# An encoder layer on one core: where w_out's right operands are split, and how the merge's weights and heads are fed

## The chip, the cores and the metric

The kernel runs on one core of one Trainium2 chip. The metric is the time of one execution on the device, in microseconds (us). Engines are called PE (TensorE matmuls; PEld is its weight load), DVE (VectorE), ACT (ScalarE), POOL (GpSimd) and SP (SyncE, which here only issues transfers).

## The reference, cut to what matters

One layer over a sequence of 1024 positions and 1024 channels, in float32: a SwiGLU feed-forward block, a mixer with two branches, a second SwiGLU block, and a final norm.

```python
def reference(x, ...):
    x = x + 0.5 * swiglu(rms_norm(x, ffn1_norm), ffn1_wg, ffn1_wu, ffn1_wd)   # D_FF = 2816
    x = x + hybrid_mixer(rms_norm(x, mix_norm), ...)
    x = x + 0.5 * swiglu(rms_norm(x, ffn2_norm), ffn2_wg, ffn2_wu, ffn2_wd)
    return rms_norm(x, final_norm)

def hybrid_mixer(h, ...):
    u_f, q, k, v, g_a, g_b = split(h @ w_in)
    y_a = fourier_branch(u_f) @ w_fourier_out          # real part of a 2-D DFT per group
    o = diff_attention(q, k, v, positions, rel_bias, lam)   # softmax(s1) - lam * softmax(s2), 4 heads
    y_b = rms_norm(o, subln_g).reshape(...) @ w_attn_out
    merged = sigmoid(g_a) * y_a + sigmoid(g_b) * y_b
    return merged @ w_out
```

## The kernel before, in words

**Products.** Every float32 matrix product is made of three passes of the array: each operand is split into a rounded high part and a low part that holds the rest, and the kernel multiplies high by high, high by low and low by high. A split is two instructions (`split`, L131 to L134): a copy into the high part on ACT (L133) and a subtraction into the low part on DVE or POOL (L134). Where a block of four by four tiles is multiplied, seven products of sums and differences take the place of eight. `seven_products` (L389) does so for projections: left operands come from a stream of weights, right operands are the normed activations that stay on chip. `Lower` (L455) does so for the products that add to the residual: the two down-projections and w_out. One of its steps is twelve matmuls of 128x512.

**The stream of weights.** `Stream` (L150) holds a list of loads and preparations in order. `get` (L180) hands out the next prepared operand and runs ahead: five loads and two preparations past the one handed out, but not past the first entry of `stops`. `stop()` puts such a mark at the end of the list as it stands, `open()` takes the first mark away. The marks are: one after the first FFN's weights (L708, opened in `done1`, L1171), one after the eight pieces of w_attn_out (L1668, opened in `done2`, L1886), one after the second FFN's weights. A prepared operand lies in a tile called op, of which there are four (L136). A loaded block lies in a tile called r2 (shown as r in the trace), of which there are fourteen. A tile is free when its last reader is done.

**Lower.** `prep` (L539) makes the two operands of one step: the left one is a sum of activations, the right one a block of weights or a sum of blocks that was put into memory earlier (`sums_d`). `land` (L511) starts the right block's load up to six steps ahead, into spare quarters of the n tiles; `prep` splits it into an operand slot. There are twelve slots, two to a step: eight halves of the tiles n2, n3, n12, n13 and four op tiles (`slots`, `open_ext` L527, `slot` L533). For w_out, `LAST` (L40) names the products whose splits subtract on POOL: left of P4, P2 and P3, right of P2; P2 and P3 are the closing ones.

**Stages.** Input norm; first up-projection (`ffn`, L825: 11 blocks of hidden columns, two times seven products of twelve matmuls each); first down-projection; projections of the mixer with heads 0 and 1 beside them; heads 2 and 3 with the Fourier branch beside them (loop at L1783, g from 18); the merge `y_b` (L1817: for each of 16 outputs, twelve matmuls against w_attn_out, then a gate); w_out (`low.run`, L1895); second up-projection and down-projection; final norm.

**Beside the first up-projection** three generators are stepped once a product. `right_sums` (L734) makes the sums of right blocks of the down-projection and then those of w_out (order given at L1164). `bias_prepare` (L987) makes the position bias. `mixer_weights` (L767) splits the Fourier weights and, one piece every five products, w_attn_out, loads and stores of 0.25 and 0.5 MB a piece; it is stepped in the third to the ninth block of hidden columns, 98 products.

**Heads and merge.** `head_prep` (L1254) loads each half of q and k twice through the tile rh (three of them) and splits it; `combine` (L1332) scales one softmax by the other's factor, on DVE for odd blocks of heads 2 and 3 and on ACT and POOL for even ones; `turn` (L1344), `weigh` (L1362), `back` (L1376) and `head_norm` (L1420) follow. In `fourier` (L1442) a DVE and an ACT instruction write the two interleaved halves of one tile, DVE first (L1559, L1561). Before the last head is normed, the first four outputs of the merge are started with the heads that are ready. Pieces of w_attn_out come as ready operands through the stream, on ACT's queue (L1661 to L1668).

**Order of the work.** A planner orders each engine's instructions when the kernel is built: it runs a simulated time line, takes the first ready instruction in program order, and gives tiles out as they come free. `in_order` pins an instruction behind the one before it on its engine. On the chip each engine then follows its list.

```python
def get(self, prep=None):
    prep = self.PREP if prep is None else prep          # 2
    self.ahead(self.used + 1, self.used + 1)
    self.ahead(self.used + 1 + self.LOAD, self.used + 1 + prep)   # LOAD = 5
```

Of the kernel before, what the change touches and what calls it, by code (L numbers as in the profile page):

```python
# [27 lines left out]
H = 4  # L28
# [8 lines left out]
FOURIER_STEPS = 40  # L37
EARLY = ("34", "156", "016", "01"), ("34", "", "016", "01"), ("4", "4", "01", "")
DRAINS = {4: {(0, 2): 1, (1, 1): 3, (1, 2): 3, (1, 3): 3}, NP: {(n, j): 1 for n in range(2) for j in range(2 - n, 11 - n, 2)}}
LAST = ("P4", "P2", "P3"), ("P2",)  # L40
NBLK = 7
HEAD_ROWS = P * (PITCH + 1) + 64
SCALE = 1.0 / np.sqrt(float(S * P))
# [5 lines left out]
def encoder_layer(ctx: ExitStack, tc: tile.TileContext, a: dict, out: bass.AP):  # L49
# [405 lines left out]
    class Lower:  # L455
# [55 lines left out]
        def land(self):  # L511

            while self.landing < min(self.prepared + self.LAND, len(self.steps)):
                c, q, j, u = self.steps[self.landing]
                name = self.ORDER[q]
                srcs = [u["right"][name]]
                if self.spills and q >= 5:
                    srcs.insert(0, u["far"][q - 5])
                if len(store[self.where(c, q)]) < len(srcs):
                    return  # L520
                self.landing += 1
                pieces = [take(self.where(c, q)) for _ in srcs]
# [16 lines left out]
        def prep(self):  # L539

            self.land()
            c, q, j, u = self.steps[self.prepared]
            self.prepared += 1
            name = self.ORDER[q]
            a = [p and p[1] for p in u["a"]]

            def add(y, op, v, w):
                dve.tensor_tensor(out=y, in0=v, in1=w, op=op)

            if name == "P1" and u["raw"]:  # L550
                add(a[2], ALU.subtract, a[0], a[2])
            if name == "P5":
                add(a[0], ALU.add, u["s"], a[0])
            pieces = self.landed.pop(0)
            if len(pieces) == 1:
                left = self.LEFT[name]
                pieces.insert(0, ("s", u["s"]) if left == "s" else u["a"][left])
            ops = []
            for (_, src), names in zip(pieces, LAST):
                key, o = self.slot(q >= 5)  # L560
                split(src, o[:, 0, :], o[:, 1, :], pool if name in names and not self.spills else dve)
                ops.append((key, (o[:, 0, :], o[:, 1, :])))
            self.ops.append(ops)
            give(pieces[1])
# [12 lines left out]
            self.pump(2)  # L577
# [176 lines left out]

    attn_d = dram.tile([DT, P, 2, 512], F32, name="attn_d")
    cx_d = dram.tile([P, 2, 512], F32, name="cx_d")
    cw_d = dram.tile([4, P, 4, 2, 256], F32, name="cw_d")
    three = {}

# [7 lines left out]
    def mixer_weights():  # L767
# [29 lines left out]
        for q in range(4):  # L797
# [15 lines left out]
                yield  # L813
                in_order(sp.dma_start(out=cw_d[q][:, 2 * i:2 * i + 2], in_=t.bitcast(F32)))
            yield
        for dm in range(DT):
            r, o = htile(dm % 2 * 2, [P, 512], F32), htile(dm % 2 * 2 + 1, [P, 2, 512])
            in_order(sp.dma_start(out=r, in_=a["w_attn_out"][dm]))
            for _ in range(4):
                yield  # L820
            parts(r, o[:, 0, :], o[:, 1, :])
            yield
            in_order(sp.dma_start(out=attn_d[dm], in_=o.bitcast(F32)))

    def ffn(k, x_src, each, beside, also=None, third=None):  # L825

# [327 lines left out]
    def each1():  # L1154
# [5 lines left out]
        if n == 9:  # L1160
            bank_list.clear()
        drain(1 if n < 9 else 2)

    low = ffn(1, a["x"], each1, right_sums([(down(1, j), sums_d[1][j]) for j in (*range(SPILL, NP), *range(SPILL))]  # L1164
                                           + [(outward(j), sums_d["o"][j]) for j in range(4)]), bias_prepare(), mixer_weights())
    state = {}

    def done1(t, x, r):
# [64 lines left out]
    def twice(src):  # L1233

        r = rh()
        for half in (L, U):
            sp.dma_start(out=r[half, :], in_=src)
        return r
# [8 lines left out]
    def k_split(h, c, hh, r):  # L1247

        hs = slice(hh * HS, (hh + 1) * HS)
        kh, kl = stk[h][2 + c][:, hs], stk[h][4 + c][:, hs]  # L1250
        in_order(act.activation(kh, r, AF.Copy))
        pool.tensor_tensor(out=kl, in0=r, in1=kh, op=ALU.subtract)

    def head_prep(h):  # L1254

        if h == 3:
            two = [ntile(4 + j, [P, 2, S]) for j in range(2)]
            stk[h] = [two[j // 2][:, j % 2, :] for j in range(4)] + [xtile(5, [P, S], F32R)]
        else:
# [10 lines left out]
        r = None  # L1270
        for fn, t in ((q_split, h), (k_split, 4 + h)):
            for hh in range(2):
                if r is not None:
                    for c in range(2):
                        due[0](h, c, due[1], r[c])
                r = [twice(proj_d[t][(L, U)[c], hh * HS:(hh + 1) * HS]) for c in range(2)]
                due = fn, hh
                yield
        for c in range(2):
            due[0](h, c, due[1], r[c])  # L1280
        r = load_v(0)
        yield
# [49 lines left out]
    def combine(g):  # L1332
# [2 lines left out]
        dve.reciprocal(out=cc, in_=l2s[:, g:g + 1])  # L1335
        dve.tensor_scalar(out=cc, in0=cc, scalar1=l1s[:, g:g + 1], scalar2=nlam, op0=ALU.mult, op1=ALU.mult)
        s1, s2 = sc[g]
        if g % 2 == 1 and g >= G0:
            dve.scalar_tensor_tensor(out=s1, in0=s2, scalar=cc, in1=s1, op0=ALU.mult, op1=ALU.add)
        else:  # L1340
            act.activation(s2, s2, AF.Copy, scale=cc)  # L1341
# [100 lines left out]
    def fourier():  # L1442
# [72 lines left out]
        for n_, j in enumerate(order):  # L1515
# [37 lines left out]
            if n_ + 1 < len(order):  # L1553
# [2 lines left out]
            af = r2()  # L1556
            af2 = af.rearrange("p (k two) -> p two k", two=2)
            q = 0 if even else 1
            dve.scalar_tensor_tensor(out=af2[:, q], in0=alt, scalar=quarter, in1=ps[:, q * 256:(q + 1) * 256],  # L1559
                                     op0=ALU.mult, op1=ALU.add)  # L1560
            act.activation(af2[:, 1 - q], ps[:, (1 - q) * 256:(2 - q) * 256], AF.Copy)  # L1561
            if j == 0:
                stack(A[0][:, 0, :], af, (A[0][:, 0, :], A[0][:, 1, :]), three["x"])
            else:
# [93 lines left out]
                    sp.dma_start(out=ya_d[dm, :, hs], in_=y)  # L1658
                yield

    def fetch_op(src):  # L1661
        o = op_tile()
        act.dma_start(out=o.bitcast(F32), in_=src)
        return o[:, 0, :], o[:, 1, :]
# [91 lines left out]
    def prefetch(n):  # L1756
# [11 lines left out]
        for k in range(n):  # L1768
            ready.append(inputs(k // 2, k % 2, where))

    fgen = fourier()
    hgen = head_prep(3)
    NG = H * TT
# [9 lines left out]
    for g in range(G0 + 2, NG + 2):  # L1783
# [28 lines left out]


    todo = [(dm, hh) for dm in range(DT) for hh in range(2)]
    wa = {}

    def y_b(n_, ps, heads):  # L1817

        dm, hh = todo[n_]
        if dm not in wa:  # L1820
            wa[dm] = ws.get()
# [8 lines left out]
    for _ in head_norm(H - 1, (0,)):  # L1830
        pass

    first4 = []
    for n_ in range(4):
        if n_ % 2 == 0:
            two = banks2()
        first4.append(two[:, n_ % 2 * 512:(n_ % 2 + 1) * 512])
        y_b(n_, first4[n_], range(H - 1))
    back(NG - 2)
    head_scale(NG - 2, NG)  # L1840
    for _ in head_norm(H - 1, (1,)):
        pass
    units = [{"a": [None] * 4, "raw": True, "right": rights(outward(j), sums_d["o"][j])} for j in range(4)]
# [6 lines left out]
    for n_, (dm, hh) in enumerate(todo):  # L1850
        while len(ready) < min(n_ + 9, len(todo)):
            ready.append(inputs(*todo[len(ready)]))
        if n_ < 4:
            ps = first4[n_]
            y_b(n_, ps, (H - 1,))
        else:
            ps = bank("bp"[n_ % 2])
# [184 lines left out]
```

## Time and profile before

| | |
|---|---|
| Median of 3 runs | 2035.76 us (2034.42 to 2037.39) |
| The profiled execution | 2035.69 us, of which the span of instructions is 2033.9 us |
| PE busy | 1953.8 us of the span (96%), 9460 matmuls |
| DVE, ACT, POOL busy | 1409.7, 1000.8, 629.8 us |
| Moved | 341.60 MB |

The span runs from the first instruction to the last; 1.8 us of the profiled execution lie around it. Busy time is the time in which an engine executes; a matmul's end is modelled. The idle time before an instruction is put down to what released it.

### The profile page before, as it was taken

Reading aid. Unit: us, or ns where it says so; the run is one execution under the profiler, and the core shown is the slowest. Engines: PE = TensorE matmul, PEld = TensorE weight load, DVE = VectorE, ACT = ScalarE, POOL = GpSimd, SP = SyncE. Lnnn points to the kernel's source line nnn. Section 1 sums busy time; section 2 is a strip of 40 time slices with the busy share of each in tenths; the row PEclk is TensorE's granted clock in tenths of the full one; section 3 lists DMA queues with packets and bytes.
Section 4 is the critical chain, followed back from the end, with each engine's and each line's share of the span. In section 5 each row is a group of like instructions: output and inputs, shape, how many; then the busy total and the mean of one; then the engine's idle time right before and its main releaser. Section 6 shows DMA issues by size and latency. Waiting matters only on the chain. (4 is left out here: it accounts for less than half of the span.)

```text
span 2033.9 us, 27633 instructions
## 1 busy us (share of the span) xinstructions
PE 1953.8 (96%) x9460; PEld 1635.3 (80%) x9460; DVE 1409.7 (69%) x2165; ACT 1000.8 (49%) x1804; POOL 629.8 (31%) x477
## 2 busy tenths in 40 slices
PE   6999999999999999999998898998999999999998
PEld 5887888888888878888886786877888888888886
DVE  7777767649767846656657886868766654578765
ACT  7434344334355645867756653356333333344454
POOL 6533223220000354344375540057322323300010
PEclk9999999999999999999999899999999999999999
DMA  4567956419426353344358668433655432166335
GB/s 135 195 211 254 318 199 224 156 50 333 145 78 214 116 163 122 119 140 139 104 162 278 194 207 301 143 104 95 211 200 189 150 119 73 53 218 227 104 102 173
DMA packets 205216, 341.60 MB, mean 168 GB/s; under 512 B 22101, under 2 KB 63069, under 8 KB 204561
## 3 DMA queue, kind: packets, MB, share of 16 engines
q1 hardware_dynamic: 197792, 324.35, 48.3%
q10 hardware_dynamic: 5760, 12.59, 1.7%
q0 software_dynamic: 1520, 2.88, 0.5%
q8 instruction: 74, 1.21, 0.3%
q14 instruction: 70, 0.57, 0.1%
HBM read 249.53 MB, written 94.40 MB: 169 GB/s over the span
## 5 line engine op out<-in xcount | busy, mean ns | idle before, releaser
L405 PE MATMUL p<-n,op 128*128 128x512 f32 (+1 forms) x5256 | 1151.5, 378 | 21.4 <-DVE op L134 7.3
L405 PEld LDWEIGHTS p<-n,op 128*128 128x128 f32 x5256 | 944.9, 190 | 207.0 <-DVE op L134 8.8
L217 POOL TENSOR_TENSOR r<-r,r 128x512 f32<-128x512 f32 x252 | 361.2, 1440 | 885.9 <-DVE op L134 507.8
L134 DVE TENSOR_TENSOR op<-r,op 128x512 fp32r<-128x512 f32 x427 | 356.9, 840 | 282.6 <-ACT op L133 271.6
L133 ACT ACTIVATE op<-r 128x512 fp32r<-128x512 f32 x446 | 277.9, 627 | 290.6 <-PE p L405 198.2
L607 PE MATMUL b<-n 128*128 128x512 f32 x996 | 237.4, 391 | 0.9 <-DVE r L1860 0.9
L607 PEld LDWEIGHTS b<-n 128*128 128x128 f32 x996 | 187.2, 188 | 40.3 <-ACT op L133 1.3
L417 ACT ACTIVATE r<-p 128x512 f32<-128x512 f32 (+1 forms) x138 | 74.1, 537 | 124.3 <-PE p L405 121.6
L607 PE MATMUL b<-op,op 128*128 128x512 f32 x528 | 129.3, 391 | 2.7 <-DVE op L134 2.7
L607 PEld LDWEIGHTS b<-op,op 128*128 128x128 f32 x528 | 99.4, 189 | 23.7 <-DVE op L134 3.1
L421 DVE TENSOR_TENSOR r<-p,r 128x512 f32<-128x512 f32 (+1 forms) x138 | 85.0, 616 | 40.3 <-PE p L405 37.0
L133 ACT ACTIVATE n<-n 128x512 fp32r<-128x512 f32 x126 | 74.7, 621 | 68.5 <-PE b L607 22.3
L134 DVE TENSOR_TENSOR n<-n,n 128x512 fp32r<-128x512 f32 x118 | 82.3, 716 | 32.1 <-ACT n L133 32.1
L607 PE MATMUL p<-n 128*128 128x512 f32 x336 | 80.1, 390 | 0.0
L1914 POOL TENSOR_TENSOR r<-r,x 128x512 f32<-128x512 f32 x5 | 7.7, 1559 | 224.3 <-ACT r L1913 224.3
L607 PEld LDWEIGHTS p<-n 128*128 128x128 f32 x336 | 62.9, 188 | 13.0
L1342 POOL TENSOR_TENSOR x<-x,x 128x1024 f32<-128x1024 f32 x16 | 38.4, 2398 | 101.4 <-ACT x L1341 101.4
L607 PE MATMUL p<-op,op 128*128 128x512 f32 x288 | 68.3, 391 | 0.0
L607 PEld LDWEIGHTS p<-op,op 128*128 128x128 f32 x288 | 53.8, 188 | 11.0
L133 ACT ACTIVATE op<-n 128x512 fp32r<-128x512 f32 x66 | 39.3, 621 | 35.3 <-PE b L607 13.9
L1327 DVE CUSTOM_DVE_ANT_0 x<-A,x 128x1024 f32<-128x1024 f32 x32 | 39.0, 1219 | 20.2 <-PE b L1358 13.4
L133 ACT ACTIVATE n<-x 128x512 fp32r<-128x512 f32 x48 | 30.0, 630 | 42.8 <-PE b L607 33.1
(336 smaller groups left out, 2454.3 us busy)
## 6 DMA issues: line engine op xcount, KB each, us to landing
kx<-in_ffn_wd SPq DMA_DIRECT2D x118, 256.0 KB
r<-in_ffn_wg SPq DMA_DIRECT2D x96, 256.0 KB
r<-in_ffn_wu SPq DMA_DIRECT2D x94, 256.0 KB
n<-sums_d SPq DMA_DIRECT2D x88, 256.0 KB
sums_d<-kx SPq DMA_DIRECT2D x66, 256.0 KB
proj_d<-r SPq DMA_DIRECT2D x56, 256.0 KB
h_d<-x SPq DMA_DIRECT2D x16, 512.0 KB
rh<-proj_d SPq DMA_DIRECT2D x64, 128.0 KB
```

The costliest lines, as they stand in the source:

```text
L133: act.activation(hi, src, AF.Copy)
L134: eng.tensor_tensor(out=lo, in0=src, in1=hi, op=ALU.subtract)
L217: pool.tensor_tensor(out=b[o], in0=b[x], in1=b[y], op=op)
L405: pe.matmul(ps, lhsT=w[wi][:, d * P:(d + 1) * P], rhs=xn[b][xi][:, d, cols], start=(first and m == 0), stop=(last and m == 11), skip_group ...
L417: act.activation(o, view(p), AF.Copy)
L421: dve.tensor_tensor(out=o, in0=view(p), in1=o, op=ALU.add)
L607: pe.matmul(ps[p], lhsT=wa[ai][:, p * P:(p + 1) * P], rhs=wb[bi], start=(j == 0 and m == 0 and name in self.FRESH), stop=False, skip_group ...
L1327: dve.tensor_tensor_reduce(out=dst, in0=ps, in1=bt, scale=-0.125, scalar=3.0e38, op0=ALU.add, op1=ALU.min, accum_out=nmx)
L1342: pool.tensor_tensor(out=s1, in0=s2, in1=s1, op=ALU.add)
L1914: pool.tensor_tensor(out=y[1], in0=y[1], in1=gain[1][1], op=ALU.mult)
```

## The change

- w_out's right operands (28: four units of seven products) are split beside the first up-projection, in `mixer_weights`, and stored as both parts in `out_d`, 0.5 MB each. In the w_out stage a right operand is loaded straight into its slot (in `prep`, on SP's queue), with no split there. All left operands of w_out are split on ACT and DVE; `LAST` goes.
- The pieces of w_attn_out and w_out, 36 in all, go through that generator one to a product, with loads two pairs ahead. So that w_out's sums are there, `right_sums` makes them first.
- w_attn_out's pieces no longer come through the stream: `fetch_wa` loads six of them in the attention loop (four into op tiles, two into x4 and kx) and the last two in the merge, on SP's queue. The stream's entries for them and the mark after them go.
- Six outputs of the merge are started before the last head is normed, in place of four.
- `head_prep`: k is loaded over its whole width into the tile where its low part will stand and split in place; q's halves and k's are split in turn.
- `combine`: for heads 2 and 3 all blocks on DVE. `fourier`: the ACT copy stands ahead of the DVE instruction.

```diff
-LAST = ("P4", "P2", "P3"), ("P2",)
@@ Lower.land
-                srcs = [u["right"][name]]
+                srcs = [] if "both" in u else [u["right"][name]]
@@ Lower.prep
-            if len(pieces) == 1:
+            if len(pieces) < 2:
...
-            for (_, src), names in zip(pieces, LAST):
+            for i in range(2):
                 key, o = self.slot(q >= 5)
-                split(src, o[:, 0, :], o[:, 1, :], pool if name in names and not self.spills else dve)
+                if i < len(pieces):
+                    split(pieces[i][1], o[:, 0, :], o[:, 1, :])
+                else:
+                    sp.dma_start(out=o.bitcast(F32), in_=u["both"][q])
                 ops.append((key, (o[:, 0, :], o[:, 1, :])))
@@ mixer_weights
-        for dm in range(DT):
-            r, o = htile(dm % 2 * 2, [P, 512], F32), htile(dm % 2 * 2 + 1, [P, 2, 512])
-            in_order(sp.dma_start(out=r, in_=a["w_attn_out"][dm]))
-            for _ in range(4):
+        jobs = [(a["w_attn_out"][dm], attn_d[dm]) for dm in range(DT)]
+        for j in range(4):
+            b = rights(outward(j), sums_d["o"][j])
+            jobs += [(b[name], out_d[j, n]) for n, name in enumerate(Lower.ORDER)]
+        def load_two(n):
+            t = htile(n % 2 * 2, [P, 2, 512], F32)
+            for q in range(2):
+                in_order(sp.dma_start(out=t[:, q, :], in_=jobs[2 * n + q][0]))
+            return t
+        ahead = [load_two(0), load_two(1)]
+        yield
+        yield
+        for n in range(len(jobs) // 2):
+            t = ahead.pop(0)
+            for q in range(2):
+                o = htile(2 * q + 1, [P, 2, 512])
+                parts(t[:, q, :], o[:, 0, :], o[:, 1, :])
                 yield
-            parts(r, o[:, 0, :], o[:, 1, :])
-            yield
-            in_order(sp.dma_start(out=attn_d[dm], in_=o.bitcast(F32)))
+                in_order(sp.dma_start(out=jobs[2 * n + q][1], in_=o.bitcast(F32)))
+            if n + 2 < len(jobs) // 2:
+                ahead.append(load_two(n + 2))
@@ head_prep, k_split
-        in_order(act.activation(kh, r, AF.Copy))
-        pool.tensor_tensor(out=kl, in0=r, in1=kh, op=ALU.subtract)
+        in_order(act.activation(kh, kl.bitcast(F32), AF.Copy))
+        pool.tensor_tensor(out=kl, in0=kl.bitcast(F32), in1=kh, op=ALU.subtract)
...
+        r = load_q(0)
+        for c in range(2):
+            twice(proj_d[4 + h][(L, U)[c], :], stk[h][4 + c].bitcast(F32))
...
@@ combine
-        if g % 2 == 1 and g >= G0:
+        if g >= G0:
@@ fourier
+            act.activation(af2[:, 1 - q], ps[:, (1 - q) * 256:(2 - q) * 256], AF.Copy)
             dve.scalar_tensor_tensor(out=af2[:, q], in0=alt, scalar=quarter, in1=ps[:, q * 256:(q + 1) * 256],
                                      op0=ALU.mult, op1=ALU.add)
-            act.activation(af2[:, 1 - q], ps[:, (1 - q) * 256:(2 - q) * 256], AF.Copy)
@@ the stream
-    for dm in range(DT):
-        ws.add(None, lambda dm=dm: fetch_op(attn_d[dm]))
-    ws.stop()
     order_ffn(2)
@@ the attention loop
+        if g == G0 + TT + 2:
+            fetch_wa(0, 1, 2, 3)
+            fetch_wa(4, 5, homes=[xtile(4, [P, 2, 512], F32R), T(big, "kx", [P, 2, 512], F32R, 2)])
@@ the merge
-    for n_ in range(4):
+    for n_ in range(6):
...
+        first.append(two[:, n_ % 2 * 512:(n_ % 2 + 1) * 512] if n_ < 4 else bank("p"))
...
+        if n_ == 3:
+            fetch_wa(6, 7)
```

where

```python
def fetch_wa(*dms, homes=None):
    for n, dm in enumerate(dms):
        o = op_tile() if homes is None else homes[n]
        sp.dma_start(out=o.bitcast(F32), in_=attn_d[dm])
        wa[dm] = o[:, 0, :], o[:, 1, :]
```

## Rows read from the trace of the kernel before

**Rows 1.** Windows: busy us (count) of PE, PEld, DVE, ACT, POOL; clock, DMA share, GB/s.

```profile
220.00:320.00 100.00, 98.98 (x434) 80.69 (x433) 68.49 (x89) 37.73 (x67) 30.04 (x21) 1.00 0.73 256
320.00:440.00 120.00, 120.00 (x531) 99.38 (x530) 77.73 (x99) 47.98 (x81) 37.78 (x26) 1.00 0.40 135
1040.00:1240.00 200.00, 178.06 (x990) 150.00 (x989) 150.12 (x281) 116.15 (x214) 100.67 (x101) 0.96 0.67 214
1240.00:1292.00 52.00, 43.22 (x183) 34.37 (x182) 39.25 (x67) 9.84 (x18) 0.00 (x0) 0.90 0.83 301
1292.00:1377.00 85.00, 81.53 (x367) 66.61 (x366) 59.40 (x83) 41.98 (x86) 32.69 (x22) 0.98 0.31 107
```

**Rows 2.** PE's time line: start, duration, line, out<-in, count [idle before <-releaser].

```profile
1073.08 4.14 PE L405 MATMUL p<-n,op 128*128 128x512 f32 x10 [3.78 <-DVE op L134]
...
1135.85 0.69 PE L1382 MATMUL b<-ident,rh 128*128 128x128 f32 x2 [8.04 <-ACT rh L1374]
...
1250.14 0.63 PE L1431 MATMUL b<-ident,rh 128*128 128x128 f32 x4 [2.27 <-DVE rh L1428]
...
1265.73 2.90 PE L1825 MATMUL b<-x,op 128*128 128x512 f32 x6 [5.17 <-DMA op<-attn_d]
...
1270.99 1.73 PE L1825 MATMUL p<-x,op 128*128 128x512 f32 x6
...
1273.94 1.52 PE L1825 MATMUL b<-x,op 128*128 128x512 f32 x6
...
1276.66 1.52 PE L1825 MATMUL p<-x,op 128*128 128x512 f32 x6
...
1362.36 1.20 PE L607 MATMUL b<-op,op 128*128 128x512 f32 x4 [2.67 <-DVE op L134]
```

**Rows 3.** The merge weights' stores and loads: durations min/median/max in ns, first and last.

```profile
L823 SPq DMA_DIRECT2D attn_d<-h x8: 326/354/417, 234.3 to 330.3; - x8
L1663 ACTq DMA_DIRECT2D op<-attn_d x8: 326/326/346, 1081.0 to 1265.2; - x8
```

**Rows 4.** Groups by line, 120 to 400 us: busy us, mean ns, idle before.

```profile
L134 DVE TENSOR_TENSOR op<-r,op 128x512 fp32r<-128x512 f32 x100 | 83.5, 836 | 48.7 <-ACT op L133 47.8
L133 ACT ACTIVATE op<-r 128x512 fp32r<-128x512 f32 x101 | 63.3, 628 | 86.7 <-PE p L405 70.0 <-issue 8.7 <-POOL r L217 7.6
```

**Rows 5.** DVE's time line in the last projection and beside the heads.

```profile
1066.97 7.25 DVE L134 TENSOR_TENSOR op<-r,op 128x512 fp32r<-128x512 f32 x3 [6.91 <-ACT op L133]
...
1129.65 4.33 DVE L134 TENSOR_TENSOR x<-r,x 128x512 fp32r<-128x512 f32 x1
1133.91 0.47 DVE L1559 SCALAR_TENSOR_TENSOR r<-r,r,p 128x256 f32<-128x256 f32 x1
```

**Rows 6.** ACT's time line: the wait for a head's load, and the merge weights' issues.

```profile
1063.04 0.63 ACT L1244 ACTIVATE x<-rh 128x512 fp32r<-128x512 f32 x1 [4.20 <-DMA rh<-proj_d]
...
1080.96 0.33 ACTq L1663 DMA_DIRECT2D op<-attn_d  x1
...
1084.12 0.33 ACTq L1663 DMA_DIRECT2D op<-attn_d  x1
```

**Rows 7.** The Fourier copy's line: its wait on ACT's queue, in ns.

```profile
L1561 ACTq EVENT_SEMAPHORE  x1: 9787/9787/9787, 1124.6 to 1124.6; - x1
```

**Rows 8.** Groups by line, 1080 to 1240 us: combine on POOL, DVE and ACT.

```profile
L1342 POOL TENSOR_TENSOR n<-n 128x1024 f32<-128x1024 f32 x8 | 19.2, 2403 | 16.2 <-ACT n L1341 16.2
...
L1339 DVE SCALAR_TENSOR_TENSOR n<-n,ccs 128x1024 f32<-128x1024 f32 x8 | 13.7, 1708 | 0.2
...
L1341 ACT ACTIVATE n<-n,ccs 128x1024 f32<-128x1024 f32 x8 | 9.2, 1148 | 0.6 <-DVE ccs L1336 0.6
```

**Rows 9.** The DVE form of combine, by its line: ns min/median/max, first and last start.

```profile
L1339 DVE SCALAR_TENSOR_TENSOR n<-n,ccs x8: 1275/1286/3075, 1092.9 to 1215.5; 128x1024 f32<-128x1024 f32 x8
```

**Rows 10.** Groups by line in the w_out stage, 1292 to 1377 us.

```profile
L134 POOL TENSOR_TENSOR op<-n,op 128x512 fp32r<-128x512 f32 x8 | 11.9, 1506 | 23.6 <-ACT op L133 23.6
...
L377 DVE SCALAR_TENSOR_TENSOR h<-h,col,x 128x512 f32<-128x512 f32 x8 | 10.3, 1356 | 0.0
```

More of the change, by code (lines that the diff above doesn't have):

```diff
@@ L558, in prep @@
             ops = []
-            for (_, src), names in zip(pieces, LAST):
+            for i in range(2):
                 key, o = self.slot(q >= 5)
-                split(src, o[:, 0, :], o[:, 1, :], pool if name in names and not self.spills else dve)
+                if i < len(pieces):
+                    split(pieces[i][1], o[:, 0, :], o[:, 1, :])
+                else:
+                    sp.dma_start(out=o.bitcast(F32), in_=u["both"][q])
                 ops.append((key, (o[:, 0, :], o[:, 1, :])))
             self.ops.append(ops)
-            give(pieces[1])
+            for piece in pieces[1:]:
+                give(piece)
             if name in ("P5", "P4", "P2", "P3") or name == "P7" and self.spills:
@@ L756, in encoder_layer @@
     cx_d = dram.tile([P, 2, 512], F32, name="cx_d")
+    out_d = dram.tile([4, NBLK, P, 2, 512], F32, name="out_d")
     cw_d = dram.tile([4, P, 4, 2, 256], F32, name="cw_d")
@@ L1162, in each1 @@
         drain(1 if n < 9 else 2)
-    low = ffn(1, a["x"], each1, right_sums([(down(1, j), sums_d[1][j]) for j in (*range(SPILL, NP), *range(SPILL))]
-                                           + [(outward(j), sums_d["o"][j]) for j in range(4)]), bias_prepare(), mixer_weights())
+    low = ffn(1, a["x"], each1, right_sums([(outward(j), sums_d["o"][j]) for j in range(4)] +
+                                           [(down(1, j), sums_d[1][j]) for j in (*range(SPILL, NP), *range(SPILL))]),
+              bias_prepare(), mixer_weights())
     state = {}
@@ L1231, in encoder_layer, with twice @@
     L, U = slice(0, 64), slice(64, 128)
-    def twice(src):
-        r = rh()
+    def twice(src, r):
         for half in (L, U):
@@ L1245, in q_split, with k_split @@
         pool.tensor_tensor(out=q[lo, :], in0=r[lo, :], in1=q[lo, :], op=ALU.subtract)
-    def k_split(h, c, hh, r):
+    def k_split(h, c, hh):
         hs = slice(hh * HS, (hh + 1) * HS)
         kh, kl = stk[h][2 + c][:, hs], stk[h][4 + c][:, hs]
-        in_order(act.activation(kh, r, AF.Copy))
-        pool.tensor_tensor(out=kl, in0=r, in1=kh, op=ALU.subtract)
+        in_order(act.activation(kh, kl.bitcast(F32), AF.Copy))
+        pool.tensor_tensor(out=kl, in0=kl.bitcast(F32), in1=kh, op=ALU.subtract)
     def head_prep(h):
@@ L1267, in load_v, with load_q @@
             return r
[L1270 to L1278, printed above, removed]
-        for c in range(2):
-            due[0](h, c, due[1], r[c])
+        def load_q(hh):
+            return [twice(proj_d[h][(L, U)[c], hh * HS:(hh + 1) * HS], rh()) for c in range(2)]
+        r = load_q(0)
+        for c in range(2):
+            twice(proj_d[4 + h][(L, U)[c], :], stk[h][4 + c].bitcast(F32))
+        yield
+        for c in range(2):
+            q_split(h, c, 0, r[c])
+        r = load_q(1)
+        yield
+        for c in range(2):
+            k_split(h, c, 0)
+        yield
+        for c in range(2):
+            q_split(h, c, 1, r[c])
         r = load_v(0)
+        yield
+        for c in range(2):
+            k_split(h, c, 1)
         yield
@@ L1659, in fourier @@
                 yield
[L1661 to L1664, printed above, removed]
-    for dm in range(DT):
-        ws.add(None, lambda dm=dm: fetch_op(attn_d[dm]))
-    ws.stop()
     order_ffn(2)
@@ L1769, in prefetch @@
             ready.append(inputs(k // 2, k % 2, where))
+    wa = {}
+    def fetch_wa(*dms, homes=None):
[3 more added lines that the diff above has]
+            wa[dm] = o[:, 0, :], o[:, 1, :]
     fgen = fourier()
@@ L1814, in encoder_layer @@
     todo = [(dm, hh) for dm in range(DT) for hh in range(2)]
-    wa = {}
     def y_b(n_, ps, heads):
         dm, hh = todo[n_]
-        if dm not in wa:
-            wa[dm] = ws.get()
         w, hs = wa[dm], slice(hh * HS, (hh + 1) * HS)
@@ L1831, in encoder_layer @@
         pass
-    first4 = []
-    for n_ in range(4):
-        if n_ % 2 == 0:
+    first = []
+    for n_ in range(6):
+        if n_ < 4 and n_ % 2 == 0:
             two = banks2()
-        first4.append(two[:, n_ % 2 * 512:(n_ % 2 + 1) * 512])
-        y_b(n_, first4[n_], range(H - 1))
+        first.append(two[:, n_ % 2 * 512:(n_ % 2 + 1) * 512] if n_ < 4 else bank("p"))
+        y_b(n_, first[n_], range(H - 1))
     back(NG - 2)
@@ L1842, in encoder_layer @@
         pass
-    units = [{"a": [None] * 4, "raw": True, "right": rights(outward(j), sums_d["o"][j])} for j in range(4)]
+    units = [{"a": [None] * 4, "raw": True, "both": out_d[j]} for j in range(4)]
     low = Lower([units], lambda r, p: p + (4 if r == 0 else 0), None, lambda c, q: "ab"[q > 3])
@@ L1852, in encoder_layer @@
             ready.append(inputs(*todo[len(ready)]))
-        if n_ < 4:
-            ps = first4[n_]
+        if n_ < len(first):
+            ps = first[n_]
             y_b(n_, ps, (H - 1,))
```

## The prediction
> **What bounds the kernel now.** I read the page's busy shares first (PE 96%), then cut the span into stages with the windows, then asked for PE's waits on its time line, and last for what the engine named there had done. The windows [rows 1] show where PE is idle: 1.0 us of 100 and 0 of 120 in the first up-projection, but 21.9 of 200 us beside heads 2 and 3 (200 - 178.06), 8.8 of 52 in the merge and 3.5 of 85 in the w_out stage. So the kernel is bound by PE except in the middle, and there a few long waits hold most of the loss [rows 2]: 3.78 us at 1073, 8.04 at 1136, 2.27 at 1250, 5.17 at 1266, 2.67 at 1362. A wait costs more than itself. The twelve matmuls behind the 5.17 us wait (1265.73 to 1270.99) take 5.26 us, twelve later on (1273.94 to 1276.66) take 2.72. The stage's granted clock is 0.90, so a fifth of its 52 us ran at 1.2 instead of 2.4 GHz [rows 1]. I count 2.5 us for the slow matmuls behind a long wait.
>
> **The change part by part**, against the profiled execution's 2035.69 us (the median of the runs is 0.07 higher).
>
> *First up-projection: +4 us.* Each right piece adds a load of 0.25 and a store of 0.5 MB, 0.786 million bytes; 28 make 22.0 MB, all 36 pieces 28.3. In 220 to 320 us 256 GB/s went with a share of 0.73 [rows 1], so a full share is 351 GB/s: 28.3 MB are 81 us of all sixteen DMA engines. The generator asks for a piece each product of 2.72 us, 98 us in all, and begins at about 220 (before, its first piece, five products into that part, was stored at 234.3 and the last at 330.3 [rows 3]). That stretch already carried 73 us of transfers, some 16 of them the seven pieces of w_attn_out that fell into it. So 57 + 81 = 138 us of transfers want to pass in about 100: 38 too many. Behind it, 320 to 440, a share of 0.60 is free, 72 us. If the pieces slide there the cost is nothing; if PE has to wait for all of it, 38. The pieces are pinned only behind what was traced before them; the weights' loads are not pinned and the planner can send them ahead. But a weight load then stands behind stores of 1.5 us each. I take 4: at 0.73 the stretch lost 1.0 us, and now some 140 us run at full share. The splits themselves, 28 x 0.836 = 23.4 us on DVE and 28 x 0.628 = 17.6 on ACT [rows 4], raise DVE from 146 to 170 of 220 us and ACT from 86 to 103 [rows 1]. They lie beside PE's products and cost nothing; without that cover a piece would cost 1.5 us. The new order of the sums moves no work: what is late is the sums of the down-projection, by four jobs, and they are read only at the stage's end.
>
> *Heads' loads: -2 us.* ACT stood 4.20 us for a load into rh [rows 6]; the splits on POOL that had waited for such loads then ran close together, by my reading, and beside them three DVE subtractions took 7.25 us [rows 5], 2.5 by the mean [rows 4]; PE waited 3.78 and ran its next ten matmuls in 4.14 instead of 2.27 us [rows 2]. With k loaded into its own place fewer loads queue for rh. The whole of it would be -5.7; if POOL stays as busy there, 0; and two loads more in that place (the stream, below) could cost 2.
>
> *Copy ahead of DVE, combine on DVE: -5 us.* ACT's queue stood 9.79 us for the Fourier copy [rows 7], until the DVE instruction in front of it had started at 1133.91 [rows 5]; ACT's next instructions, one of which PE awaited for 8.04 us [rows 2], were queued behind it. Put first, the copy waits for PE alone; DVE then waits for it, 0.4 us, with its splits queued behind. DVE itself is late next: its 4.33 us subtraction ended only there [rows 5]. So 8.0 + 2.5 is the upper end of the gain and I take half. Combine takes 8 x 2.4 = 19.2 us from POOL and 9.2 from ACT [rows 8] and adds eight DVE instructions, 10.3 us at the median of 1.286 [rows 9]: DVE goes from 150 to 160 of 200 us, still under PE's 178. Eight at the mean of 1.708 are 13.7 [rows 8]; were DVE the bound here, the 3.4 between would be the loss. Those are the ends: -10.5 and +3.4.
>
> The same instruction takes 1.275 us at best and 3.075 at worst [rows 9], with POOL at work beside it. The Trainium skill's page "SBUF — State Buffer", section "SBUF: two separate sides", says that a DVE instruction with two SBUF inputs and a GpSimd one that reads SBUF take a lock in turns: "the other fully blocks". By it each moved combine may stand behind one POOL instruction, and the price is the mean, 3.4 us of DVE more than the sum has; by the median row it is nothing. The 4.33 us subtraction [rows 5], 3.5 over the mean of its kind [rows 4], agrees with such blocking.
>
> *Merge: -5 us.* If all pieces of w_attn_out were there, the 5.17 us wait with its slow matmuls (-7.7) and most of the 2.27 (two more outputs, 18 matmuls of 0.227, are 4.1 us of cover) would go: -10. But the diff also takes away the mark in the stream. At the last projection the stream prepares two entries ahead; before, these were two pieces of w_attn_out, at 1080.96 and 1084.12 [rows 6]. Now the next entries are the second FFN's first weights: two of the four op tiles and four r2 tiles are held from there until that FFN starts, 300 us later. Then `fetch_wa(0, 1, 2, 3)` finds two op tiles, pieces 2 and 3 can load only when 0 and 1 are used up, and outputs five and six can't be started early. Pieces 4 and 5 have homes of their own and can fill that time. I take half the gain; the other end is +2, a second wait for pieces 2 and 3 as long as the old one with nothing won.
>
> *w_out stage: +1 us.* 28 copies leave ACT (17.6 us), 16 subtractions leave POOL, some 24 us (eight of them 11.9 [rows 10]), and of DVE's subtractions 24 go and 12 come. The wait of 2.67 stood behind eight norm instructions that took 10.3 us [rows 10]; with POOL out of the way it goes, with some slow matmuls: -3.7. Against it, a right operand now comes after its slot is free, and the four op slots have two tiles: a step on them must wait until the step before it is done, load 0.5 MB and only then run. The wait for such a load was 5.17 us under traffic [rows 2], 1.5 is the transfer alone. Of the five such places in 28 steps the planner can put other steps of the same product in front in all but one, I reckon: +4.7. The ends are -3.7 and +20.
>
> Sum: 4 - 2 - 5 - 5 + 1 = -7: **2028.7 us**.
>
> **The rivals.**
> *The slots are not short* (the stream stops, or the tiles come free in time): 4 - 4 - 7 - 10 - 3.7 = -20.7, 2015 us. For it: every one of these waits has a named cause that the change removes. Against: the entries are consecutive in the list and nothing is between them. 0.25.
> *Slower: the transfers set the pace of the up-projection.* Place: 220 to 360 us. Two or three prepared operands cover some 8 us, the two pairs loaded ahead 5; of the 38, 25 fall on PE in place of 4. 2028.7 + 21 = 2050. It decides from 15 us on, where the 11 of the other parts are eaten up and 4 more. For it: ACT executes its list in order, so one late piece holds the weights' copies behind it. Against: 72 us of free share right behind. 0.15.
> *The w_out stage starves* at all five places: +20 instead of +1, 2048 us. For it: each such step needs both tiles. Against: its matmuls can be put behind others. 0.12.
> *The gains are given back at the next wait*: beside the heads DVE and PE are close (160 against 178), so a wait that goes lets the next one grow; +4 and -6 leave 2034. 0.13.
>
> **How the numbers follow.** The forecast has 0.35, with a range of its own of 2020 to 2037. The range to hold 8 in 10: 2011 to 2048; it leaves out the lower part of the first rival and the upper halves of the two slow ones, under 0.2. About 0.2%, 4 us, is what a measurement of this kernel can tell from no change. Faster: 0.25 + 0.31 of the forecast = 0.56. Within: 0.13 + 0.04 = 0.17. Slower: 0.15 + 0.12 = 0.27.
>
> **What would show it.** The windows of 220 to 440 us: share near 1 for some 140 us, and PE's idle time there, which is the first term. The start of the loads of the second FFN's gate weights: near 1070 if the stream runs on, after the merge if not. ACT's wait at the Fourier copy: gone or not. The merge's pieces: when 2 and 3 are loaded. PE's waits in the w_out stage, and whether they are for a right operand's load. I am wrong if PE stays full up to 1040 and the merge's waits go whole (under 2018), or if the up-projection grows by over 15 us.

## The result, and the profile after: slower, not faster

The changed kernel took 2055.18 us (median of 4 runs, 2053.00 to 2057.68) against 2035.09 of the kernel before beside it: ratio 1.0090, 95% interval 1.0076 to 1.0104. Measured again later it took 2051.72 us, ratio 1.0085 (1.0068 to 1.0102). The forecast was 2028.7, in a range that ended at 2048.

Where the time went is read from five marks on PE's time line: the first down-projection's first matmul, the last weighing of a head, the first w_out matmul, the second FFN's first matmul, the end. Each number is one mark's start less the one before it, in us, of one profiled execution. In the changed kernel the first of the last weighing's 24 matmuls stands 0.65 us ahead of the others; its mark is the second one:

```
                            before   after  after again  forecast of the change
to the first down-proj.     461.85  474.19     468.21       +4
on to the last weighing     779.79  763.55     763.72       -2 and -5
merge                        49.72   56.69      56.39       -5
w_out stage                  85.66  104.43     104.55       +1
second FFN to the end       656.88  656.94     656.93        0
sum                        2033.90 2055.80    2049.80
```

So +12.3 (again: +6.4), -16.2, +7.0 and +18.8. The part beside the heads gained twice what was forecast; the merge and the w_out stage, forecast at -4 together, cost 25.8.

The windows of the changed kernel, with the columns of [rows 1], the last two from the last weighing and the first w_out matmul on:

```profile
220.00:320.00 100.00, 96.42 (x423) 78.82 (x422) 76.02 (x96) 47.11 (x83) 29.24 (x20) 1.00 0.93 331
320.00:440.00 120.00, 115.44 (x494) 94.31 (x493) 81.89 (x113) 51.92 (x90) 37.64 (x25) 0.97 0.73 258
1040.00:1240.00 200.00, 185.19 (x1034) 156.09 (x1034) 159.47 (x297) 111.48 (x211) 97.04 (x100) 0.97 0.66 213
1237.74:1294.43 56.69, 44.58 (x189) 35.15 (x190) 33.86 (x59) 7.05 (x14) 1.66 (x1) 0.85 0.65 220
1294.43:1398.86 104.43, 89.90 (x368) 72.10 (x369) 53.55 (x83) 31.81 (x65) 8.50 (x7) 0.90 0.55 188
```

Against [rows 1], PE now idles 3.6 of 100 and 4.6 of 120 us in the up-projection (1.0 and 0 before), 14.8 of 200 beside the heads (21.9 before), 12.1 in the merge (8.8 before) and 14.5 in the w_out stage (3.5 before). PE's time line names the waits in the last two:

```profile
1246.23 1.09 PE L1459 MATMUL b<-ident,rh 128*128 128x128 f32 x4 [2.27 <-DVE rh L1456]
...
1258.86 2.93 PE L1855 MATMUL p<-x,op 128*128 128x512 f32 x6 [7.83 <-DMA op<-attn_d]
...
1268.96 1.52 PE L1855 MATMUL b<-x,x 128*128 128x512 f32 x6
...
1328.73 5.46 PE L610 MATMUL b<-op,op 128*128 128x512 f32 x12 [3.30 <-DMA op<-out_d]
...
1351.40 4.58 PE L610 MATMUL b<-op,op 128*128 128x512 f32 x12 [3.38 <-DMA op<-out_d]
...
1378.45 2.89 PE L610 MATMUL b<-op,op 128*128 128x512 f32 x12
...
1387.30 5.39 PE L610 MATMUL b<-op,op 128*128 128x512 f32 x12 [4.21 <-DMA op<-out_d]
```

The 5.17 us wait of the merge [rows 2] is 7.83 now, and in the w_out stage, where ten of the 28 right operands go through op slots, PE waits three times for such a load: 10.9 us. Twelve matmuls right behind such a wait take 4.6 to 5.5 us, twelve with none in front 2.9. SP's time line shows what came first:

```profile
1076.49 0.91 SPq L145 DMA_DIRECT2D r<-in_ffn_wg  x2
1081.88 1.14 SPq L145 DMA_DIRECT2D r<-in_ffn_wg  x2
1117.86 0.37 SPq L1797 DMA_DIRECT2D x<-attn_d  x1
1120.94 0.32 SPq L1797 DMA_DIRECT2D kx<-attn_d  x1
1148.56 0.32 SPq L1797 DMA_DIRECT2D op<-attn_d  x1
1159.64 1.27 SPq L1797 DMA_DIRECT2D op<-attn_d  x1
1252.29 14.47 SPq L1797 DMA_DIRECT2D op<-attn_d  x3
1273.69 0.32 SPq L1797 DMA_DIRECT2D op<-attn_d  x1
```

The second FFN's gate weights are loaded at 1076, where the stream before issued the merge's weights [rows 6]. Of the four merge pieces meant for op slots at once, two are issued by 1160; the next issues at 1252, some 92 us later. Pieces 4 and 5, which have homes of their own (x and kx), are issued at 1118 and 1121, but PE first reads one of them at 1268.96 (`b<-x,x`), behind the wait.

### The profile page after: what moved, and what is told of

It is laid out like the page before. It is cut to its first block, busy times and chain, and to the rows that moved or that the text cites. A ratio compares the mean times of both kernels' runs of the same rounds, so it can differ in the third digit from the quotient of the medians.

```text
span 2055.8 us, 27682 instructions
## 1 busy us (share of the span) xinstructions
PE 1962.3 (95%) x9460; PEld 1640.3 (80%) x9460; DVE 1425.2 (69%) x2189; ACT 1003.0 (49%) x1804; POOL 595.1 (29%) x453
## 3 DMA queue, kind: packets, MB, share of 16 engines
q0 software_dynamic: 1520, 2.88, 0.4%
## 5 line engine op out<-in xcount | busy, mean ns | idle before, releaser
L610 PE MATMUL b<-op,op 128*128 128x512 f32 x528 | 135.0, 404 | 10.9 <-DMA op<-out_d 10.9
L132 ACT ACTIVATE n<-n 128x512 fp32r<-128x512 f32 x108 | 65.1, 622 | 89.3 <-PE b L610 31.9
L133 DVE TENSOR_TENSOR n<-n,n 128x512 fp32r<-128x512 f32 x108 | 73.7, 696 | 36.9 <-ACT n L132 36.9
L132 ACT ACTIVATE op<-n 128x512 fp32r<-128x512 f32 x56 | 33.7, 622 | 45.0 <-PE b L610 15.4
L133 DVE TENSOR_TENSOR op<-n,op 128x512 fp32r<-128x512 f32 x56 | 37.4, 686 | 23.5 <-ACT op L132 23.5
L785 DVE TENSOR_TENSOR h<-h,h 128x512 fp32r<-128x512 f32 (+1 forms) x45 | 41.1, 915 | 16.0 <-ACT h L784 15.7
```

The costliest lines, as they stand in the source:

```text
L132: act.activation(hi, src, AF.Copy)
L133: eng.tensor_tensor(out=lo, in0=src, in1=hi, op=ALU.subtract)
L610: pe.matmul(ps[p], lhsT=wa[ai][:, p * P:(p + 1) * P], rhs=wb[bi], start=(j == 0 and m == 0 and name in self.FRESH), stop=False, skip_group ...
L785: in_order(dve.tensor_tensor(out=lo, in0=src, in1=hi, op=ALU.subtract))
```

## The experiments

**The mark in the stream, put back.** The theory: the stream, with no mark after the mixer, prepares two of the second FFN's operands and so holds two of four op tiles through both stages. The rival: right operands that are loaded only when a slot comes free are late, however many slots there are.

```diff
+    ws.stop()
     order_ffn(2)
```

> The changed kernel with the stream's mark put back ahead of the second FFN's weights, so that the four op tiles are free in the merge and in the w_out stage. If held slots cost both stages (the slot theory): the merge, 7.0 us longer than before in the changed kernel, comes out 0 to 7 us shorter than before; the w_out stage, 104.4 us in the changed kernel, goes to 82 to 88; the up-projection keeps its +12; the whole near 2055 - 7 to 14 - 17 to 22 = 2019 to 2031. If it is the late loads of the right operands as such (each is asked for only when its slot is free): the w_out stage stays at 100 or more, only the merge gains, and the whole is near 2045 to 2050.

Measured: 2015.29 us, ratio to the kernel before 0.9908 (0.9892 to 0.9925). One line more takes 36 to 40 us off. From the last weighing to the second FFN:

```profile
1233.45:1273.35 39.90, 36.43 (x174) 29.52 (x172) 32.27 (x59) 5.70 (x11) 0.00 (x0) 1.00 0.78 285
1273.35:1354.62 81.27, 80.11 (x369) 66.14 (x369) 51.27 (x80) 32.09 (x66) 8.57 (x6) 1.00 0.71 245
```

The merge is 16.8 us shorter and the w_out stage 23.2. Part of the 16.8 is work that has moved: 54 of the merge's 192 matmuls run ahead of the last weighing here and in the kernel before, 36 in the changed kernel. The other 18, 4.1 us at 0.227, stood in the merge there; the stretch up to the last weighing is 2.5 us longer with the mark. Of the 23.2, 13.4 are PE's idle time (14.5 to 1.2) and 9.8 its busy time (89.90 to 80.11, by 369 matmuls instead of 368): the matmuls that ran at 1.2 instead of 2.4 GHz behind the waits, clock 0.90 against 1.00. The merge pieces and the right operands are there early:

```profile
1133.80 6.60 SPq L1798 DMA_DIRECT2D op<-attn_d  x3
1148.48 1.20 SPq L1798 DMA_DIRECT2D op<-attn_d  x1
1248.94 0.80 SPq L1798 DMA_DIRECT2D op<-attn_d  x2
1260.72 0.43 SPq L563 DMA_DIRECT2D op<-out_d  x1
1276.59 0.32 SPq L563 DMA_DIRECT2D op<-out_d  x1
```

The same ten late loads into slots are there; no PE wait for them is left. The rival falls.

**Only half of the mark.** It stops loads (four r2 tiles, traffic) and splits (two op tiles). Here the loads go ahead and the splits are held:

```diff
-            while self.prepared < min(prep, end):
+            while self.prepared < min(prep, end, self.hold):
...
+    ws.hold = len(ws.loads)
     order_ffn(2)
...
             ws.open()
+            ws.hold = 10 ** 6
```

> The changed kernel with the mark for one half of the stream only: the second FFN's first weights are still loaded 300 us early, into the same four r2 tiles, but not split, so that the four op tiles are free in the merge and in the w_out stage. If the op tiles alone cost both stages: merge 40 and w_out stage 81 us as with the mark, the whole 2013 to 2018. If the early loads or the r2 tiles that they hold cost them: 57 and 104 us, the whole near 2051. If both have a share: between, with the w_out stage's right loads back near their time and the merge's inputs late.

Measured: 2014.35 us, ratio 0.9908 (0.9891 to 0.9925), merge 39.7, w_out stage 81.2. The early loads are still there, and the op slots are free (SP's time line, then the windows of both stages):

```profile
1070.79 0.91 SPq L145 DMA_DIRECT2D r<-in_ffn_wg  x2
1076.28 1.14 SPq L145 DMA_DIRECT2D r<-in_ffn_wg  x2
1144.04 1.27 SPq L1799 DMA_DIRECT2D op<-attn_d  x3
```

```profile
1232.30:1271.96 39.66, 36.42 (x174) 29.52 (x172) 32.24 (x59) 6.84 (x13) 0.57 (x1) 1.00 0.81 289
1271.96:1353.19 81.23, 80.07 (x368) 66.15 (x369) 51.06 (x80) 30.97 (x64) 6.70 (x5) 1.00 0.68 232
```

This settles it: the two held op tiles, not the early loads, make both stages long.

**w_out's right operands as before**, without and with the mark:

```diff
-            jobs += [(b[name], out_d[j, n]) for n, name in enumerate(Lower.ORDER)]
+            jobs += []
...
-    units = [{"a": [None] * 4, "raw": True, "both": out_d[j]} for j in range(4)]
+    units = [{"a": [None] * 4, "raw": True, "right": rights(outward(j), sums_d["o"][j])} for j in range(4)]
```

> The changed kernel with w_out's right operands as before: loaded raw and split in the w_out stage, so that the first up-projection splits and stores only the eight pieces of w_attn_out; the mark stays away. If the 28 pieces' transfers and splits cost the up-projection its 12.3 us: the start of the first down-projection comes back to 462 to 465 us. The slot theory gives the merge the same +7 as in the changed kernel, and the w_out stage between: no load of a right operand into a slot, but still two op tiles, 86 to 95 us; the whole is 2055 - 10 to 12 - 9 to 18 = 2025 to 2036. If the late loads alone made the w_out stage long, slots or not, it goes back to 86 and the whole to 2025.

> Both: the mark put back and w_out's right operands as before. What is left of the change is the heads' loads, the Fourier copy and combine, the merge's pieces fetched ahead and the order of the sums. Up-projection +0 to 3 against before, projections and heads -16, the merge -7 to 0, w_out stage -4 to +1: 2036 - 16 - 4 - 2 = near 2014, from 2009 to 2022. If the 16 us gained beside the heads hang on the second FFN's weights being loaded early (a mixer that finds fewer transfers beside it), half of them go with the mark: 2020 to 2028.

Measured: 2030.19 us without the mark (0.9975, 0.9965 to 0.9986) and 2014.78 with it (0.9906, 0.9889 to 0.9922). The up-projection is back within 1.1 and 0.6 us of before. With two slots held the merge is late with or without the 28 pieces (59.3 us); the w_out stage takes 91.2 us, 5.6 more than before, and 5.8 come back behind it (its second FFN takes 651.0 us from its first matmul, 656.9 before and in the changed kernel; no run shows why). The 28 pieces cost the w_out stage 13 us more (104.4), but only with two slots held; with four they make it 0.9 us shorter (81.3 against 82.2). All in all, splitting them ahead is worth nothing here: 2015.29 against 2014.78.

**What the up-projection pays for.** The same kernel once more, then without the 28 stores (from the changed kernel), without the 28 splits and with a slower pace (both with the mark):

```diff
 e5  -                sp.dma_start(out=o.bitcast(F32), in_=u["both"][q])
     +                sp.dma_start(out=o.bitcast(F32), in_=attn_d[q])
     ...
     -                in_order(sp.dma_start(out=jobs[2 * n + q][1], in_=o.bitcast(F32)))
     +                if 2 * n + q < DT:
     +                    in_order(sp.dma_start(out=jobs[2 * n + q][1], in_=o.bitcast(F32)))
 e6  +                if 2 * n + q < DT:  (around the two lines that split; the others store t)
 e7        if n + 2 < len(jobs) // 2:
              ahead.append(load_two(n + 2))
     +     yield
```

> The changed kernel once more, unaltered, with a second profiled execution: it tells which differences between single profiles are those of the execution. The first down-projection began at 474.2 us in its first profile and at 467.4 in the kernel with the mark put back, which issues the same instructions up to there. If executions scatter there, it comes out between 466 and 474 and the term of the up-projection is 5 to 12 us; if the 12.3 us are the kernel's own, it is at 474 again. Merge 57 and w_out stage 104 us again in either case.

> The changed kernel without the 28 stores of the split right operands (14.7 MB); the loads and splits beside the up-projection stay, and the w_out stage loads blocks of the same size from attn_d instead, so what it computes is not w_out. If transfers set the pace of the up-projection: its +12.3 us falls to 0 to 4, the whole is near 2045. If the splits on ACT and DVE set it: it stays at +10 to 12, the whole near 2054.

> The changed kernel with the mark put back (2015.3 us) and without the splits of the 28 right pieces on ACT and DVE: the raw block is stored twice in their place, the same bytes, so what the w_out stage computes is not w_out. If the splits, with the work of ACT and DVE that stands behind them, cost the up-projection its 5.5 us: the first down-projection begins at 462 to 463 instead of 467.4. If the transfers do: it stays at 466 to 468. Without the 28 stores it was at 468.8, which speaks against the stores but not against the loads.

> The changed kernel with the mark put back and one pause more of the generator for each pair of pieces, so that it asks for three products' time per pair instead of two. If the pieces' crowding costs the up-projection 5.5 us: 2 to 4 of them go, the whole is 2011 to 2013. If the cost is the same wherever the pieces lie in that stage: 2015 again, within 2.

Measured: 2051.72 (changed kernel again), 2050.11 without the stores (1.0074, 1.0056 to 1.0092), 2009.86 without the splits (0.9871, 0.9855 to 0.9888), 2014.60 with the slower pace (0.9897, 0.9880 to 0.9913). The stage ends at 468.2, 468.8, 466.2 and 466.6 us. So the 12.3 us of the first profile are partly that execution's: its clock in 320 to 440 us was 0.97, 1.00 in the others, and 467.4 to 468.8 is what three other kernels with the same instructions up to there show. 200 to 440 us, in the changed kernel again, without the stores, without the splits and before:

```profile
200.00:440.00 240.00, 233.46 (x1021) 190.58 (x1020) 176.29 (x232) 106.77 (x185) 76.85 (x51) 1.00 0.82 289
```

```profile
200.00:440.00 240.00, 233.60 (x1024) 191.52 (x1025) 174.39 (x232) 107.54 (x186) 76.03 (x53) 1.00 0.68 229
```

```profile
200.00:440.00 240.00, 234.57 (x1030) 192.50 (x1029) 152.69 (x206) 92.79 (x159) 72.54 (x51) 1.00 0.82 289
```

```profile
200.00:440.00 240.00, 238.98 (x1051) 196.62 (x1050) 162.31 (x210) 94.40 (x162) 73.86 (x51) 1.00 0.59 199
```

The DMA share falls from 0.82 to 0.68 without the stores and PE's idle time stays at 6.4 us (6.5 with them): not the stores. Without the splits DVE does 24 us less and PE idles 5.4 us (5.1 in the kernel with the mark, which has the splits): this profile does not show the cost to be theirs, though the median of the runs is 5.4 us lower than with them (the profiled execution, 2015.7 us, was the longest of the four). The pace is not it. Which part of the 5 to 7 us belongs to the splits, and which to the loads and the order of the generator, stays open.

**The parts beside the heads, alone on the kernel before.**

```diff
 b1  -            dve.scalar_tensor_tensor(out=af2[:, q], ...)
                  act.activation(af2[:, 1 - q], ps[:, (1 - q) * 256:(2 - q) * 256], AF.Copy)
     +            dve.scalar_tensor_tensor(out=af2[:, q], ...)
 b2  as the change's own twice, k_split and head_prep
 b3  -        if g % 2 == 1 and g >= G0:
     +        if g >= G0:
 b4  b2 and b3;  b5  b1, b2 and b3
```

> The kernel before with one part of the change alone: ACT's Fourier copy ahead of DVE's instruction. If that copy is behind most of the 16 us gained beside the heads: ACT's 9.8 us wait and PE's 8.04 us wait are gone and the whole is 2035 - 8 to 12 = 2023 to 2027. If the wait only moves to the next late engine there (DVE's long subtractions): 0 to -4, 2031 to 2035.

> The kernel before with one part of the change alone: k loaded into its own place and split there. If the loads into rh made the 3.78 us wait of PE and the slow matmuls behind it: -4 to -7, 2028 to 2031. If POOL stays as busy there: 0, near 2035. If this part carries most of the 16 us: 2023 or less.

> The kernel before with one part of the change alone: combine of the last two heads wholly on DVE. If POOL was what made DVE's subtractions long beside the heads (4.3 to 7.3 us): they shorten and the whole is 2035 - 4 to 10 = 2025 to 2031. If DVE is near its bound there: 0 to +4, 2035 to 2039.

> The kernel before with two parts of the change: the heads' loads and combine on DVE. Alone they gave -5.4 and -4.1 us. If they add up: 2025.5, from 2023 to 2028. If the one takes away what the other would gain, the last wait beside the heads being one of DVE's: 2029 or more. If they help each other: 2022 or less.

> The kernel before with all three parts beside the heads: the heads' loads, combine and the swap. With the swap, which alone cost 4 us and in the changed kernel with the mark gave 1.1: if its cost is still there, 2027 to 2031; if combine has taken it away, 2022 to 2026. The rest, down to 2015, is then the merge's pieces fetched ahead.

Measured: swap 2038.61 us (1.0017, 1.0004 to 1.0031), heads' loads 2028.99 (0.9975, 0.9965 to 0.9986), combine 2030.30 (0.9985, 0.9975 to 0.9995), heads and combine 2022.48 (0.9950, 0.9932 to 0.9968), all three 2024.62 (0.9949, 0.9936 to 0.9961). Heads' loads and combine carry the gain, some 10 us; the swap carries none of it. With the swap alone ACT's wait at the copy falls from 9.8 [rows 7] to 3.9 us, and this comes in its place (time line, rows of POOL, DVE and PE):

```profile
1127.67 2.26 POOL L1474 TENSOR_TENSOR r<-r,r 128x511 f32<-128x511 f32 x1
...
1128.73 7.07 DVE L134 TENSOR_TENSOR n<-r,n 128x512 fp32r<-128x512 f32 x1
...
1134.00 1.25 POOL L1252 TENSOR_TENSOR kx<-rh,n 128x512 fp32r<-128x512 f32 x1
...
1136.49 1.09 PE L1358 MATMUL b<-ident,n 128*128 128x128 f32 x4 [5.92 <-DVE oss L1390]
```

One DVE subtraction of 7.07 us, while POOL runs without a gap from 1127.67 to 1135.25. The wait moved on, to the kind of subtraction that was already long before (4.33 us [rows 5]). With combine off POOL and the k loads out of rh no DVE instruction from 1060 to 1140 us took over 2 us, and combine itself stays at the median of [rows 9] (1282 ns, 1286 there) with 1929 ns at worst (3075 there). In the changed kernel it is dearer, 1476 and 2300 ns. First the row of this kernel (heads and combine), then that of the changed kernel:

```profile
L1346 DVE SCALAR_TENSOR_TENSOR n<-n,ccs x16: 1274/1282/1929, 1073.6 to 1207.0; 128x1024 f32<-128x1024 f32 x16
```

```profile
L1367 DVE SCALAR_TENSOR_TENSOR n<-n,ccs x16: 1277/1476/2300, 1085.2 to 1213.6; 128x1024 f32<-128x1024 f32 x16
```

**The swap undone**, with the mark, and the same with the right operands as before:

```diff
-            act.activation(af2[:, 1 - q], ps[:, (1 - q) * 256:(2 - q) * 256], AF.Copy)
             dve.scalar_tensor_tensor(out=af2[:, q], ...)
+            act.activation(af2[:, 1 - q], ps[:, (1 - q) * 256:(2 - q) * 256], AF.Copy)
```

> The changed kernel with the mark put back (2015.3 us) and the Fourier copy behind DVE's instruction again, as before. The swap alone, on the kernel before, gave +3.5 us. If the order decides nothing once combine has left POOL and ACT (in the kernel with combine alone on DVE, ACT never stood at that copy): 2015 again, within 2. If the swap costs here as it did alone: 2010 to 2013. If the copy in front is what keeps ACT from standing there: 2018 to 2024, with ACT's long wait back.

> The same without the swap, with w_out's right operands loaded raw and split in the w_out stage as before. With the swap these two kernels were 0.5 us apart: an up-projection 5 us shorter, and 3 us more in the merge and the w_out stage. If that holds: within 2 us of the kernel beside it; the two together tell the swap's worth, 2009 to 2016 if it is 0 to 5 us.

Measured: 2016.42 (0.9905, 0.9888 to 0.9921) and 2016.92 us (0.9911, 0.9894 to 0.9927): 1 to 2 us over the same kernels with the swap, no difference that can be told. Once combine is on DVE, no effect of the order can be told. Every version that computes w_out and has the op tiles free, by mark or by hold, lies near 2015 us, 0.9 to 1.0% under the kernel before and some 1.8% under the changed one.

## Why the prediction was wrong

*The step that failed: what the held op tiles cost.* The mechanism stood in the prediction: the mark is dropped, the stream runs on, two op tiles and four r2 tiles are held from about 1076 us on. The trace shows just that. Its price was set at 5 us in the merge (half of the gain, with +2 as the end) and 4.7 in the w_out stage. It is 16.8 and 23.2, 40 us instead of 10 (37.5 when the 2.5 us that the stage before is shorter by are taken off). Three things in the pricing were wrong.

In the merge I let pieces 4 and 5, in homes of their own, fill the time until 2 and 3 are loaded. They were there in time, but in PE's order their matmuls stand behind those of the late pieces, and nothing filled it: the 7.83 us wait took the place of the 5.17 that the early fetch was to remove [rows 2]. I also put no price on the 18 matmuls that could no longer run ahead of the last weighing. Without the held tiles the fetch gives 9.8 us, my upper end of 10, but the sum behind that end was partly luck: the 5.17 us wait goes, 1.8 of the 2.27 stay (the kernel before already ran 54 matmuls ahead, and the two more outputs add none), and PE's busy time falls by 4.5 us (40.94 to 36.43 by 174 matmuls) where I had 2.5.

In the w_out stage I reckoned with one wait for such a load, the planner putting other steps in front elsewhere; PE waited three times, 10.9 us.

And I added the waits without what comes behind them, though I had counted 2.5 us of slow matmuls for each of the long waits of before. In the w_out stage PE's busy time is 9.8 us longer than with the tiles free. The twelve matmuls behind the three waits hold 6.8 of it (2.6, 1.7 and 2.5 over 2.88), twelve behind a wait of 2.32 us for DVE another 1.7. The rival "the w_out stage starves" (+20) had the size right for that stage (+18.8), and got 0.12; but it counted five waits and no slow matmuls, so that the number came out is in part luck. None of the rivals had the merge slower than before.

*The rival "the slots are not short" (2015 us) was the kernel with the mark.* Its terms were 4, -11 (heads and swap), -10 and -3.7; measured in that kernel 5.5, -13.7, -9.8 and -4.4, at 2015.29 us. So with the tiles free that sum was near, and the tiles decide between it and the changed kernel.

*First up-projection, +4:* right in its size, 5 to 7 us in four executions and 12.3 in one. The DMA share stood between 0.89 and 1.01 from 200 to 360 us, as forecast, the pieces slid (the last store at 379.0 us), and PE lost little. But the share of the transfers in it is not what I argued: without the stores the idle time is the same.

*Heads and combine, -7:* the gain was 16.2, in the kernel with the mark 13.7; the difference is no gain, since 18 of the merge's matmuls (4.1 us) had only moved behind the last weighing. My ends reached -16.2 (-5.7 and -10.5), so the half that I took was too cautious, and the cause within it was the wrong one: I gave the swap the main part; alone it gave nothing, and combine with the heads' loads gave 10 us (11.6 in that stage of its profile; the 2 left of 13.7 no run assigns). ACT's 9.79 us wait [rows 7] ended with the end of the DVE instruction, at 1134.4, and not with its start, as I had read it. ACT still waits 3.27 us for a load into rh in the changed kernel (at 1066.86; 4.20 in [rows 6]), so that wait is not what went; DVE's long subtractions [rows 5] are: none in the changed kernel takes over 2.4 us from 1040 to 1240. The Trainium skill's lock ("SBUF — State Buffer", section "SBUF: two separate sides") I had used to price the combines that move to DVE. I left out what follows from it, though the page does not say it: less work on POOL would free what DVE has there already. Combine alone, with 19.2 us of POOL's work [rows 8] gone and 10.3 added to DVE, came out 3 to 4 us faster, and the 4.33 us subtraction took 1.46. That fits, but the lock itself was not tested, and ACT lost 9.2 us of work with it.

*The second FFN, 0:* 0.06 us.

## What to carry to other kernels

A mark or stop in a prefetch stream is a statement on buffers: before it is removed, count which tiles the entries behind it will hold, until when, and who shares their pool in between. Price a short pool by every load that must pass through what is left of it, and add the slow matmuls behind each wait to the wait. A tile that is ready early helps only if the engine's order reads it early. A wait whose engine has another late engine beside it can move when it is removed, as with the swap alone; with the late engine's load taken away, both went here.

## What the runs showed of the hardware

One 128x512 subtraction on DVE, 0.68 us elsewhere, took 7.07 us while POOL had eight instructions back to back; it ended 0.55 us after the last of POOL's tensor-tensor instructions in that stretch. By the section of the Trainium skill's page "SBUF — State Buffer" named above, the engine that starts first keeps the ports for its whole instruction and the other blocks until it finishes; here the record of DVE's instruction spans seven of POOL's that began after it. The 4.33 us one of before [rows 5] ended 0.54 us after such a stretch of POOL.

Two profiled executions of the same program differ by 6.0 us in one stage of 474 us, the up-projection, and agree within 0.4 us in the other four: a difference of that size in a single profile is not yet one of the kernel.
